# A heads' scores as three fp32r passes on row halves, a longer planned power in the opening, and new job orders

## The chip, the cores and the metric

One core of one Trainium2 chip runs the whole program. The metric is the device time of one execution in microseconds (us); lower is better. Engines are named as in the profile: PE is TensorE (its weight loads are listed apart as PEld), DVE is VectorE, ACT is ScalarE, POOL is GpSimd, SP is the engine that issues the DMAs here.

## What is computed

Two layers of a hybrid encoder on 256 rows of 1024 features, in fp32. Each layer mixes tokens by two kinds of attention with gates, then runs a squared-ReLU MLP. The change touches the scores of the first kind ("A": 8 query heads over 2 key heads, head dimension 64):

```python
def gqa_attention(q, k, v):
    ...
    q = q.reshape(B, S, Hkv, rep, hd)
    scale = hd ** -0.5
    def block(i):
        qi = lax.dynamic_slice_in_dim(q, i * Q_BLOCK, Q_BLOCK, axis=1)
        s = jnp.einsum('bqgrd,bkgd->bgrqk', qi, k, preferred_element_type=jnp.float32) * scale
        p = jax.nn.softmax(s, axis=-1).astype(v.dtype)
        return jnp.einsum('bgrqk,bkgd->bqgrd', p, v)

for l in range(DEPTH):
    ada = c_act @ w_ada[l] + b_ada[l]
    sh1, sc1, gt1, sh2, sc2, gt2 = [a[:, None, :] for a in jnp.split(ada, 6, axis=-1)]
    h = rms(x, g_mix[l]) * (1.0 + sc1) + sh1
    parts = jnp.split(h @ w_in[l], IN_SPLITS, axis=-1)
    qa = axial_rope(rms(qa, q_norm_a[l]), row_cs, col_cs)
    ka = axial_rope(rms(ka, k_norm_a[l]), row_cs, col_cs)
    y_a = gqa_attention(qa, ka, va) @ w_branch_a[l]
    ...
    x = x + gt1 * (mixed @ w_out[l])
    h2 = rms(x, g_mlp[l]) * (1.0 + sc2) + sh2
    x = x + gt2 * (jnp.square(jax.nn.relu(h2 @ w_ff1[l])) @ w_ff2[l])
```

## The kernel before

The program first records every operation with its engine, tiles and an assumed cost (`Plan.record`, `Plan.cost`, L259 to L330), then plays the list through a model of the engines (`Plan.run`, L427) and issues everything in the order of the planned start times (`Plan.issue`, L661). Each engine works its own list in that order; waits between engines are semaphores. So an assumed cost decides only the order, and where two operations of one engine stand, not how long they take.

Weights come by DMA in tiles of 128x1024 (`wr`, 7 buffers). Each is split into a high part, rounded to the type fp32r by an ACT copy, and a low part, the remainder, by a DVE subtraction (`split_next`, L815). A product of two such pairs is three fp32r matmuls, high*high, low*high and high*low (`mm3`, L837). Most of the large products run in this way.

A layer's mixer runs a list of jobs, a string `seq0` or `seq1` (L38, L39): `c` a chunk of the q, k, v projection with its normalisation and rotation (`qk_post`, L962), `u` and `v` one eighth each of the gates, `a` and `b` a step of attention A or B, `y` a quarter of A's output projection, and `w` one tile of the adaptive vectors `ada`. A `w` is one DMA of 512 KB into `wr` and one DVE reduction of 128x1024 with its accumulator read (`ada_tile`, L742); it has no work for PE. `ada_f0` and `ada_f1` say how many such tiles follow each block of the MLP.

`qk_post` ends with PE transposes of a chunk into PSUM, which one ACT copy writes into the tile of transposed queries and keys (`dst`). For A these are `qa` (half of a buffer of the class `b8`, which has 16 buffers, L41) and `ka`. `att_a_scores` (L1099) then multiplies: two pairs of heads j, two row blocks t and two halves g give eight fp32 matmuls in a group, each with 64 contracted rows (g picks partitions 0 to 63 or 64 to 127), 128 query columns as weights and 256 key columns moving. There are two such groups in each layer. The class `b8` holds the split weights too, so its buffers bound how far ahead weights are split.

In the opening, `step_x` (L1634) normalises the two row blocks: sums of squares, one DVE addition, a power -0.5 on POOL, then the scaling on ACT or DVE and PE transposes. A DVE addition ahead of the power is planned 400 ns longer than it is (`keep(HOLD)`).

Of the kernel before, what the change touches and what calls it, by code (L numbers as in the profile page):

```python
# [12 lines left out]
F32 = mybir.dt.float32  # L13
F32R = mybir.dt.float32r
BF16 = mybir.dt.bfloat16
AF = mybir.ActivationFunctionType
ALU = mybir.AluOpType
# [3 lines left out]
P = 128  # L21
D = 1024
S = 256
DEPTH = 2
HD = 64
# [8 lines left out]
CFG = dict(ahead0=1,  # L34
  post0=(5, 2, 1, 0), s2k=9, ahead=1, last="k",
  hk=2,
  ada_f0=[3, 1, 8, 2, 1, 6, 2, 4, 2], ada_f1=[2, 0, 0, 0, 0, 0, 0, 0, 0],
  seq0="w a v w v w w c3 c4 w w v a a w u u w w v a w w w w w b w v b w w w w w w w u y w y y y w w".split(),  # L38
  seq1="u w c4 v a w w w w w u a c3 w v a c5 u w w w w w w c2 w a w y y y y u b b v w w w w w w w w v w".split())  # L39
WR = 7  # L40
NB8 = 16  # L41
WARM = 5
# [114 lines left out]
class Plan:  # L157
# [101 lines left out]
    def record(self, e, op, a, k):  # L259
# [20 lines left out]
        o["port"] = from_sbuf and op != "reciprocal" and k.get("op") != ALU.pow and "reduce" not in op.replace("tensor_tensor_reduce", "")  # L280
        self.ops.append(o)

    @staticmethod
    def division(out, lhs):

        return ("row" if lhs.ap[0][1] == HD else "") + ("col" if out.ap[0][1] == HD else "")

    @staticmethod
    def cost(e, op, outs, ins, k):

        free = lambda z: int(np.prod([c for _, c in z.ap][1:]))
        n = max(free(z) for z in outs[:1] + ins)
        if e == "PE":
            n = free(outs[0])
            if op == "matmul" and F32R not in (ins[0].dtype, ins[1].dtype):
                if n > 256 and ins[0].ap[0][1] == P:
                    return 1.7 * n, 1.7 * n + 250.0
                cut = Plan.division(outs[0], ins[0])
                if not cut:
                    return 225.0, 475.0  # L300
                occ = max(0.4175 * n, 30.0) if cut == "rowcol" else 0.835 * n
                return occ, occ + 250.0
            occ = 228.5 if n > 256 else 120.5 if n > 128 else 109
            return occ, occ + 205
        if e == "SP":
            size = max(free(z) * mybir.dt.size(z.dtype) * z.ap[0][1] for z in outs)
            row = free(outs[0]) * mybir.dt.size(outs[0].dtype)
            return 480, size * (1.8 if ins[0].ap[0][0] == 0 else 1.6 if row < 4096 else 1.0)
        if e == "POOL":
            occ = 400 + 155 * n if k.get("op") == ALU.pow else 440 + 1.7 * n  # L310
            return occ, occ + (100 if n > 4 else 60)
        bank = "PSUM" in str(ins[0].space) if ins else False
        if e == "ACT":
            occ = (52 if bank else 93) + 0.834 * n
            occ += 96 * sum(pattern(k.get(z)) is not None for z in ("bias", "scale"))
            if k.get("accum_out") is not None:
                return occ + 93, occ + 308
            return occ, occ + 150
        if n <= 16:
            return 79, 204  # L320
        if op == "tensor_copy":
            occ = 69 + n / 0.96 if bank else 68 + n * 0.521
        elif op == "tensor_scalar":
            occ = (187 if bank else 135) + n * (1.04 if bank else 0.521)
        else:
            occ = 69 + n / 0.96
        if op == "tensor_tensor_reduce":
            return occ + 6, occ + 191
        return occ, occ + 125
# [366 lines left out]
def encoder(ctx: ExitStack, tc: tile.TileContext, a: dict, out: bass.AP):  # L696
# [5 lines left out]
    act, dve, pool, pe, sp = plan.lanes()  # L702
# [14 lines left out]
    def f32(t):  # L717
        return t.bitcast(F32)
# [243 lines left out]
    def qk_post(l, c, t, ps, nh, segs, axial, dst):  # L962
        n = nh * HD
        nm = f"{l}_{c}_{t}"

        qs = s2k(f"qs{nm}")[:, :n]
        act.activation(qs, ps[:, :n], AF.Copy)
        sq = s2k(f"sq{nm}")[:, :n]
        act.activation(sq, ps[:, :n], AF.Square)
        t1 = s2k(f"t1{nm}")[:, :n]  # L970
        t2 = s2k(f"t2{nm}")[:, :n]
        v3 = lambda z: z.rearrange("p (h d) -> p h d", d=HD)
        s0, ns = segs
        per = nh // ns
        tb = tabs_of[l]
        ct = tb[:, t, 0, s0 : s0 + ns, :]
        st = tb[:, t, 1, s0 : s0 + ns, :]
        v4 = lambda z: z.rearrange("p (s h d) -> p s h d", s=ns, d=HD)
        bc = lambda z, w: z[:, :, None, :].to_broadcast([P, ns, per, w])
        if axial:  # L980
            assert ns == 1
            w = HD // 4
            q5, o5 = (z.rearrange("p (h b s x) -> p h b s x", b=2, s=2, x=w) for z in (qs, t2))
            sv = st[:, 0, :].rearrange("p (b s x) -> p b s x", b=2, s=2)
            for s in range(2):
                (dve if l == 1 else pool).tensor_tensor(
                    o5[:, :, :, s, :], q5[:, :, :, 1 - s, :],
                    sv[:, None, :, s, :].to_broadcast([P, nh, 2, w]), op=ALU.mult,
                )
        else:  # L990
            w = HD // 2
            for s in range(2):
                (dve if l == 1 else pool).tensor_tensor(
                    v4(t2)[:, :, :, s * w : (s + 1) * w], v4(qs)[:, :, :, (1 - s) * w : (2 - s) * w],
                    bc(st[:, :, s * w : (s + 1) * w], w), op=ALU.mult,
                )
        r = tl("sbuf", [P, 8], F32, "rstd", 4, f"rstd{nm}")[:, :nh]
        dve.reduce_sum(r, v3(sq), axis=AX.X)
        with plan.together():
            dve.tensor_scalar(r, r, HD * EPS, None, op0=ALU.add)  # L1000
            dve.tensor_tensor(v4(t1), v4(ps[:, :n]), bc(ct, HD), op=ALU.mult)
        pool.tensor_tensor(r, r, half[:, :nh], op=ALU.pow)
        dve.tensor_tensor(t1, t1, t2, op=ALU.add)
        dve.tensor_tensor(v3(t1), v3(t1), r[:, :, None].to_broadcast([P, nh, HD]), op=ALU.mult)
        np_ = nh // 2
        tp = pt(f"qT{nm}")[:, : np_ * P]
        for j in range(np_):
            pe.transpose(tp[:, j * P : (j + 1) * P], t1[:, j * P : (j + 1) * P], ident)
        tv = tp.rearrange("p (j n) -> p j n", j=np_)
        act.activation(dst[:, :, t * P : (t + 1) * P], tv, AF.Copy)  # L1010

    def v_post(ps, dst):
        pv = ps.rearrange("p (h d) -> p h d", d=HD)
# [17 lines left out]
    def attention_tiles(l):  # L1031
        T = {}

        z = [tl("sbuf", [P, 2, 4, S], F32, "b8", NB8, f"qk{l}{i}") for i in range(2)]
        T["qa"] = z[0][:, 0]
        T["b", 0], T["b", 1], T["b", 2] = z[0][:, 1], z[1][:, 0], z[1][:, 1]
        T["ka"] = tl("sbuf", [P, 1, S], F32, "ka", 1, f"ka{l}")
        v = tl("sbuf", [P, 2, 16, HD], F32, "b8", NB8, f"v{l}")
        T["va"] = [v[:, t, 12:14] for t in range(2)]
        T["vb"] = [v[:, t, 0:12] for t in range(2)]  # L1040
        T["oa"] = Split([tl("sbuf", [P, 4, 2, S], F32R, "b8", NB8, f"oa{l}")], 4)
        T["ob"] = Split([tl("sbuf", [P, 4, 2, S], F32R, "b8", NB8, f"ob{l}")[:, :2]], 2)
        return T
# [55 lines left out]
    def att_a_scores(l, T, js):  # L1099

        sps = {(j, g): pa(f"sa{l}_{g}_{j}") for j in js for g in range(2)}
        with plan.together():
            for j in js:
                for t in range(2):
                    for g in range(2):
                        rows = slice(HD * g, HD * (g + 1))
                        q = T["qa"][rows, j, t * P : (t + 1) * P]
                        pe.matmul(sps[j, g][:, t * S : (t + 1) * S], q, T["ka"][rows, 0, :], start=True, stop=True)
        return sps

    def att_a_soft(l, j, sps, home):
# [522 lines left out]
    def step_x(t):  # L1634
        for c in range(2):
            sum_sq(0, 0, t, c, eng[f"ss{t}{c}"] == "d")
        ss = ss_of[0, 0, t]
        r = ss[:, 0:1]
        with plan.keep(HOLD):
            dve.scalar_tensor_tensor(r, r, EPS, ss[:, 1:2], op0=ALU.add, op1=ALU.add)  # L1640
        pool.tensor_tensor(r, r, half[:, :1], op=ALU.pow)
        for g in range(2):
            xn = s2k(f"xn00{t}{g}")
            xg = x[:, t, g * 512 : (g + 1) * 512]
            if eng[f"xn{t}{g}"] == "a":
                act.activation(xn, xg, AF.Copy, scale=r)
            else:
                dve.tensor_scalar(xn, xg, r, None, op0=ALU.mult)
            ps = pt(f"xT00{t}{g}")
            for k in range(4):  # L1650
                pe.transpose(ps[:, k * P : (k + 1) * P], xn[:, k * P : (k + 1) * P], ident)
            copy_by(
                eng[f"xT{t}{g}"], xT[:, 4 * g : 4 * g + 4, t * P : (t + 1) * P], ps.rearrange("p (k n) -> p k n", k=4)
            )
# [190 lines left out]
```

## Time and profile before

| | us |
|---|---|
| median of 3 runs (727.13 to 727.39) | 727.33 |
| the profiled execution, its own time | 726.78 |
| its span in the trace | 725.0 |
| PE busy | 720.1 |
| DVE busy | 584.6 |
| ACT busy | 466.9 |
| POOL busy | 65.6 |

The profiled execution took 726.78 us, 1.78 us of it outside the traced span, and lies 0.55 us under the median. Busy is the time in which at least one instruction of the engine is in flight; overlapping instructions count once. A group's mean is the time of one instruction from start to end, so for pipelined matmuls it is longer than the step from one to the next. Nearly all operations were recorded by one helper, so all stand under one line of code, L692, and the tile names tell them apart: `w` is a split weight, `hT` the transposed activations, `ka,qk` A's scores, `qk` B's scores, `s2k` a scratch tile, `ps` PSUM.

### The profile page before, as it was taken

The numbers are of one execution on the slowest core, as the hardware profiler recorded it, in microseconds if no ns is written. First come the engines' busy times: TensorE is split into PE (matmuls) and PEld (weight loads), VectorE is DVE, ScalarE is ACT, GpSimd is POOL, SyncE is SP. The second block draws the span as 40 slices with busy tenths as digits, with TensorE's granted clock in tenths as the row PEclk, the third lists the DMA queues.
The fourth block names the chain that finished last, engine by engine and source line by source line (L and its number), as shares of the span: only waits on it lengthen the run. The fifth ranks groups of instructions, "written<-read, shape, count | busy, mean of one in ns | idle before, by whom it ended". The sixth has DMA issues, their size and how long they took to land.

```text
span 725.0 us, 10593 instructions
## 1 busy us (share of the span) xinstructions
PE 720.1 (99%) x3844; PEld 599.6 (83%) x3844; DVE 584.6 (81%) x911; ACT 466.9 (64%) x791; POOL 65.6 (9%) x60
## 2 busy tenths in 40 slices
PE   9999999999999999999999999999999999999998
PEld 7787887788888888888888888878888888888887
DVE  6999999999899978774799979898799765456643
ACT  6569589875575766653476498658847766545540
POOL 1007460000000041000003101010000000000000
PEclk9999999999999999999999999999999999999999
DMA  9997758997499998785546777968476965566101
GB/s 352 407 407 247 247 184 292 344 391 224 148 333 398 384 350 285 278 297 186 203 149 228 263 221 268 332 225 299 147 235 225 335 210 166 170 230 212 50 0 59
DMA packets 50868, 180.95 MB, mean 250 GB/s; under 512 B 5728, under 2 KB 6784, under 8 KB 50816
## 3 DMA queue, kind: packets, MB, share of 16 engines
q1 hardware_dynamic: 50816, 180.28, 70.3%
q8 instruction: 30, 0.49, 0.3%
q14 instruction: 22, 0.18, 0.1%
HBM read 178.66 MB, written 1.06 MB: 248 GB/s over the span
## 4 chain that ended last, share of the span: by engine, by line
PE 92%; DVE 4%; DMA 1%; ACT 1%; issue 1%; POOL 0%; SPq 0%; ACTq 0%; DVEq 0%
PE ps L692 92%; DVE s2k L692 2%; DVE w L692 1%; DMA wr<-in_w_x 1%; DMA xin<-in_x 1%; ACT s2k L692 0%; ACT hT L692 0%; POOL ss L692 0%; ACT w L692 0%; DVE shg L692 0%; DVE w20wx L692 0%; DVE hT L692 0%; DVE xT L692 0%; DVE rstd L692 0%; DVE xin L692 0%
## 5 line engine op out<-in xcount | busy, mean ns | idle before, releaser
L692 DVE TENSOR_TENSOR w<-wr,w 128x1024 fp32r<-128x1024 f32 x234 | 282.1, 1226 | 44.1 <-ACT w L692 43.9
L692 ACT ACTIVATE w<-wr 128x1024 fp32r<-128x1024 f32 x234 | 242.0, 1057 | 86.9 <-PE ps L692 48.9
L692 PE MATMUL ps<-w,hT 128*128 128x512 f32 x1032 | 246.0, 394 | 0.3 <-DVE s2k L692 0.3
L692 PEld LDWEIGHTS ps<-w,hT 128*128 128x128 f32 x1032 | 190.8, 188 | 40.8 <-DVE s2k L692 0.7
L692 PE MATMUL ps<-w,hid 128*128 128x512 f32 (+1 forms) x780 | 176.0, 385 | 0.0
L692 PEld LDWEIGHTS ps<-w,hid 128*128 128x128 f32 x780 | 143.1, 188 | 28.3
L692 PE MATMUL ps<-hT,w 128*128 128x512 f32 (+1 forms) x896 | 158.6, 337 | 0.0
L692 PEld LDWEIGHTS ps<-hT,w 128*128 128x128 f32 x896 | 139.4, 190 | 18.7
L692 DVE CUSTOM_DVE_ANT_0 s2k<-wr,c_act 128x1024 bf16<-128x1024 f32 x96 | 116.7, 1226 | 3.3 <-DMA wr<-in_w_ada 3.3
L692 ACT ACTIVATE s2k<-ps 128x256 f32<-128x256 f32 (+3 forms) x108 | 45.0, 439 | 70.4 <-PE ps L692 70.2
L692 DVE TENSOR_TENSOR s2k<-ps,s2k 128x256 f32<-128x256 f32 x56 | 22.9, 419 | 32.2 <-ACT s2k L692 32.1
L692 PE MATMUL ps<-w,mT 128*128 128x512 f32 x192 | 45.7, 393 | 0.0
L692 ACT ACTIVATE s2k<-s2k 128x512 f32<-128x512 f32 (+1 forms) x62 | 38.5, 623 | 7.0 <-DVE s2k L692 6.1
L692 PEld LDWEIGHTS ps<-w,mT 128*128 128x128 f32 x192 | 35.5, 188 | 7.4 <-DVE mT L692 0.3
L692 POOL TENSOR_TENSOR rstd<-rstd,half 128x8 f32<-128x8 f32 (+1 forms) x20 | 31.5, 1577 | 98.4 <-DVE rstd L692 98.1
L692 DVE TENSOR_TENSOR hid<-s2k,hid 128x512 fp32r<-128x512 f32 x28 | 19.3, 688 | 18.8 <-ACT hid L692 18.8
L692 ACT ACTIVATE pr<-pr,st 128x256 f32<-128x256 f32 (+1 forms) x64 | 32.5, 568 | 2.9 <-DVE st L692 2.9
L692 POOL TENSOR_TENSOR ss<-ss,half 128x1 f32<-128x1 f32 x8 | 5.8, 727 | 259.4 <-DVE ss L692 259.4
L692 PEld LDWEIGHTS ps<-xin,s2k 128*128 128x128 f32 x180 | 20.9, 140 | 7.1 <-issue 1.6
L692 PE MATMUL ps<-xin,s2k 128*128 128x128 f32 x180 | 26.2, 275 | 0.5 <-ACT s2k L692 0.5
L692 DVE TENSOR_TENSOR s2k<-ps,gtb 128x512 f32<-128x512 f32 (+1 forms) x18 | 11.7, 658 | 18.4 <-PE ps L692 18.4
L692 POOL TENSOR_TENSOR s2k<-s2k,tabs 128x256 f32<-128x256 f32 (+1 forms) x20 | 18.0, 919 | 52.7 <-ACT s2k L692 52.5
(106 smaller groups left out, 506.8 us busy)
## 6 DMA issues: line engine op xcount, KB each, us to landing
wr<-in_w_ff SPq DMA_DIRECT2D x120, 512.0 KB, 4.9
wr<-in_w_ada SPq DMA_DIRECT2D x96, 512.0 KB, 5.3
wr<-in_w_gate SPq DMA_DIRECT2D x32, 512.0 KB, 5.1
wr<-in_w_qkv SPq DMA_DIRECT2D x24, 512.0 KB, 4.8
wr<-in_w_x SPq DMA_DIRECT2D x16, 512.0 KB, 5.8
wr<-in_w_out SPq DMA_DIRECT2D x16, 512.0 KB, 5.5
wr<-in_w_y SPq DMA_DIRECT2D x8, 512.0 KB, 5.5
wr<-in_w_ba SPq DMA_DIRECT2D x8, 512.0 KB, 5.4
```

The lines of the kernel that those rows point to most:

```text
L692: getattr(self.real[o["e"]], o["op"])(*map(real, o["a"]), **{n: real(z) for n, z in o["k"].items()})
```

## The change

Three edits, and new job lists. First, A's queries and keys are stored as high and low fp32r parts: after the ACT copy of the transposes (now into fp32r) a DVE subtraction writes the remainder, and each score matmul becomes three fp32r matmuls, alternating between the two halves. `qa` becomes a whole `b8` buffer of its own, where it was half of one; the second half of `qk`'s second buffer stands empty. Second, the plan takes 61 ns for an fp32r matmul on part of the array, and 900 ns more for the power of the second row block in the opening. Third, the lists of jobs differ: `seq0` has 24 `w` in place of 25, `ada_f0` sums to 26 in place of 29, `seq1` has 29 in place of 24, `ada_f1` 1 in place of 2. In `seq0` the two `b` stand with two `w` between them, where a `w` and a `v` stood.

```diff
@@ CFG
-  ada_f0=[3, 1, 8, 2, 1, 6, 2, 4, 2], ada_f1=[2, 0, 0, 0, 0, 0, 0, 0, 0],
-  seq0="w a v w v w w c3 c4 w w v a a w u u w w v a w w w w w b w v b w w w w w w w u y w y y y w w".split(),
-  seq1="u w c4 v a w w w w w u a c3 w v a c5 u w w w w w w c2 w a w y y y y u b b v w w w w w w w w v w".split())
+  ada_f0=[4, 1, 9, 3, 1, 2, 0, 5, 1], ada_f1=[1, 0, 0, 0, 0, 0, 0, 0, 0],
+  seq0="w a v v w w c3 c4 w w a v u a w w v a w w u w w b w w b w w v w w w w w w w y y w y w y u".split(),
+  seq1="w u w w c4 w w v a u w a c3 w w w w v w a w w w c5 u c2 a w u w y w w y y w y w w w w b b v v w w w w w w".split())
@@ Plan
+    def slow_power(self, ns):
+
+        o = self.ops[-1]
+        o["occ"], o["lat"] = o["occ"] + ns, o["lat"] + ns
+
@@ Plan.cost
             occ = 228.5 if n > 256 else 120.5 if n > 128 else 109
+            if op == "matmul" and Plan.division(outs[0], ins[0]):
+                occ = 61.0
             return occ, occ + 205
@@ qk_post
-        act.activation(dst[:, :, t * P : (t + 1) * P], tv, AF.Copy)
+        if dst.shape[1] == 2 and len(dst.shape) == 4:
+            hi, lo = (dst[:, i, :, t * P : (t + 1) * P] for i in range(2))
+            act.activation(hi, tv, AF.Copy)
+            dve.tensor_tensor(lo, tv, f32(hi), op=ALU.subtract)
+        else:
+            act.activation(dst[:, :, t * P : (t + 1) * P], tv, AF.Copy)
@@ attention_tiles
-        T["qa"] = z[0][:, 0]
-        T["b", 0], T["b", 1], T["b", 2] = z[0][:, 1], z[1][:, 0], z[1][:, 1]
-        T["ka"] = tl("sbuf", [P, 1, S], F32, "ka", 1, f"ka{l}")
+        T["b", 0], T["b", 1], T["b", 2] = z[0][:, 0], z[0][:, 1], z[1][:, 0]
+        T["qa"] = tl("sbuf", [P, 2, 4, S], F32R, "b8", NB8, f"qa{l}")
+        T["ka"] = tl("sbuf", [P, 2, 1, S], F32R, "ka", 1, f"ka{l}")
@@ att_a_scores
-                    for g in range(2):
-                        rows = slice(HD * g, HD * (g + 1))
-                        q = T["qa"][rows, j, t * P : (t + 1) * P]
-                        pe.matmul(sps[j, g][:, t * S : (t + 1) * S], q, T["ka"][rows, 0, :], start=True, stop=True)
+                    for n, (u, v) in enumerate(((0, 0), (1, 0), (0, 1))):
+                        for g in range(2):
+                            rows = slice(HD * g, HD * (g + 1))
+                            q, k = T["qa"][rows, u, j, t * P : (t + 1) * P], T["ka"][rows, v, 0, :]
+                            pe.matmul(sps[j, g][:, t * S : (t + 1) * S], q, k, start=n == 0, stop=n == 2)
@@ step_x
         pool.tensor_tensor(r, r, half[:, :1], op=ALU.pow)
+        if t == 1:
+            plan.slow_power(900.0)
```

## Rows read from the trace of the kernel before

**Rows 1.** Page, part 1: engine, busy us (share of the span), instructions
```profile
PE 720.1 (99%) x3844; PEld 599.6 (83%) x3844; DVE 584.6 (81%) x911; ACT 466.9 (64%) x791; POOL 65.6 (9%) x60
```
**Rows 2.** Chain that ended last, its end: start us, us, what
```profile
57.21 0.69 DVE s2k L692
57.90 0.04 issue
57.95 663.97 PE ps L692 x3584
```
**Rows 3.** Waits of PE from 58 us on: us in total, times, longest
```profile
PE ps L692 <- DVE s2k L692: 0.3, 1, 0.3
```
**Rows 4.** Timeline of PE, first score group: start us, us, instruction, count
```profile
82.89 1.18 PE L692 MATMUL ps<-w,hT 128*128 128x512 f32 x4
84.00 2.00 PE L692 MATMUL ps<-ka,qk 64*128 64x256 f32 x16
85.93 0.96 PE L692 MATMUL ps<-w,hT 128*128 128x512 f32 x3
...
84.53 1.25 PE L692 MATMUL ps<-ka,qk 64*128 64x256 f32 x10
```
**Rows 5.** Groups by form, whole span: busy us, mean ns of one
```profile
L692 PE MATMUL ps<-ka,qk 64*128 64x256 f32 x64 | 8.0, 389 | 0.0
...
L692 ACT ACTIVATE qk<-ps 128x512 f32<-128x512 f32 x16 | 9.4, 599 | 7.4 <-PE ps L692 7.3
...
L692 DVE TENSOR_TENSOR mT<-ps,mT 128x512 fp32r<-128x512 f32 x8 | 5.3, 681 | 0.0
...
L692 ACT ACTIVATE mT<-ps 128x512 fp32r<-128x512 f32 x8 | 4.7, 597 | 3.6 <-PE ps L692 3.5
...
L692 PEld LDWEIGHTS ps<-s2k,xin 64*128 64x128 f32 x16 | 1.1, 187 | 0.4
...
L692 DVE TENSOR_TENSOR s2k<-ps,tabs 128x128 f32<-128x128 f32 x4 | 1.1, 280 | 0.0
```
**Rows 6.** Timeline of PE, fp32r matmuls of 256 columns on the whole array
```profile
211.39 2.30 PE L692 MATMUL ps<-hT,w 128*128 128x512 f32 x17
213.53 0.86 PE L692 MATMUL ps<-w,hid 128*128 128x512 f32 x3
```
**Rows 7.** Timeline of PE's weight loads in the opening, fp32 on halves
```profile
8.34 0.42 PEld L692 LDWEIGHTS ps<-s2k,xin 64*128 64x128 f32 x6
```
**Rows 8.** Busy time by stretch: window, its us, PE, PEld, DVE, ACT, POOL, clock, DMA
```profile
58.00:126.00 68.00, 68.00 (x371) 55.23 (x375) 67.14 (x110) 54.96 (x120) 31.12 (x28) 1.00 0.72 238
126.00:160.00 34.00, 34.00 (x275) 26.78 (x268) 32.77 (x63) 27.84 (x51) 0.00 (x0) 1.00 0.96 364
160.00:190.00 30.00, 30.00 (x145) 24.66 (x144) 28.65 (x44) 17.91 (x28) 0.56 (x1) 1.00 0.72 232
380.00:440.00 60.00, 60.00 (x290) 49.40 (x289) 53.45 (x97) 40.68 (x79) 12.65 (x8) 1.00 0.72 244
440.00:520.00 80.00, 80.00 (x526) 64.61 (x525) 67.95 (x120) 59.43 (x113) 3.37 (x3) 1.00 0.74 261
```
**Rows 9.** Waits of ACT, whole span: us in total, times, longest
```profile
ACT w L692 <- PE ps L692: 48.9, 31, 3.9
```
**Rows 10.** Timelines of the opening: POOL's powers, DVE beside them, ACT behind
```profile
7.34 1.02 POOL L692 TENSOR_TENSOR ss<-ss,half 128x1 f32<-128x1 f32 x1 [6.90 <-DVE ss L692]
9.02 1.47 POOL L692 TENSOR_TENSOR ss<-ss,half 128x1 f32<-128x1 f32 x1 [0.67 <-DVE ss L692]
...
8.86 1.22 DVE L692 CUSTOM_DVE_ANT_0 s2k<-wr,c_act 128x1024 bf16<-128x1024 f32 x1
...
10.53 1.34 ACT L692 ACTIVATE s2k<-xin,ss 128x512 f32<-128x512 f32 x2 [0.44 <-POOL ss L692]
```
**Rows 11.** Busy time of the opening's stretch, columns as in rows 8
```profile
4.00:54.00 50.00, 49.47 (x234) 39.40 (x234) 45.81 (x87) 32.71 (x49) 2.49 (x2) 1.00 1.02 408
```
**Rows 12.** Timelines of PE, attention B's scores: one of layer 0's two, layer 1's
```profile
137.14 1.56 PE L692 MATMUL ps<-qk 64*64 64x256 f32 x48
...
493.86 2.89 PE L692 MATMUL ps<-qk 64*64 64x256 f32 x96
```

## The prediction

> **What bounds the kernel now.** I read the page's busy times first, then the end of the chain of waits, then PE's waits, then busy time by stretch. PE is busy 720.1 of 725.0 us [rows 1], the chain's last 664 us are PE alone with no other engine between [rows 2], and from 58 us on PE waits once, 0.3 us [rows 3]. So time is saved only where PE's own work gets shorter, or before 58 us. The view by stretch warns of a second limit. In layer 0's attention, 58 to 190 us, DVE is busy 67.14 of 68, 32.77 of 34 and 28.65 of 30 us: 3.44 us are left. In layer 1's, 380 to 520 us, 18.6 of 140 are left [rows 8]. The opening, 4 to 54 us, has its DMA engines full (a share of 1.02 at 408 GB/s) beside a PE busy 49.47 of 50 [rows 11].
>
> **The scores, PE's part.** A group is 16 records for eight fp32 matmuls, and from its first start to that of the next matmul 1.93 us pass [rows 4]. Inside, ten records last 1.25 us and one lasts 0.389 [rows 4, 5]; so their starts lie within 0.86 us, and taken as five pairs (one per half at a time) that is 4 steps of 0.215 us. Eight pairs take 1.72 us; the other 0.21 us is the change to the halves, which the new group pays too, as do its neighbours. The new group has 24 fp32r matmuls, 12 pairs. No row shows fp32r on halves. On the whole array, the first of the 17 matmuls takes up to 0.227 us of the 2.14 from its start to the next line's, and the 16 fp32r matmuls of 256 columns behind it take 0.12 each [rows 6]. If the halves run side by side as they do in fp32, a pair takes 0.12 and the group 1.44: 0.28 saved. There are four groups (64 records [rows 5]): 1.1 us. The bounds: half of fp32's step, 0.108, saves 1.7 us; a pair that stays at fp32's 0.215 because something other than the moving columns sets it costs 12 x 0.215 - 1.72 = 0.86 a group, 3.4 us more than before. I take 0.12, since it is the same type and the same columns.
>
> What could hold the step at 0.215 is the loading of weights, since each short matmul brings a load of its own. In the opening, six loads of 64 rows by 128 columns last 0.42 us and one lasts 0.187 [rows 5, 7]: starts within 0.23 us, three pairs, two steps of 0.11 us. So two loads a step of 0.11 are possible, in fp32. The Trainium skill, on the page "TensorE: Matmul & The Clock Gate", section "LDWEIGHTS (loading the stationary operand)", speaks against the change here: a load costs columns / 1.2 ns whatever the number of rows, an estimate of 107 ns for 128 columns, and if the two loads of a pair ran one behind the other, that would be 213 ns a pair: the scores would take as long as the second rival below says, and the sum would be its 730.6 us. The 0.11 us step disagrees with loads in a row, and for fp32r on halves no run here shows it.
>
> **The remainders, DVE's part.** `qk_post` runs twice (t) for the q chunk and twice for the k chunk in each layer. Its ACT copy into fp32r costs what the fp32 copy costs (597 and 599 ns [rows 5]). New are four subtractions of 128x512 at 681 ns, from the same form, and four of 128x128 at 280 ns, the nearest form [rows 5]: 3.84 us of DVE, 1.92 in each layer. In layer 0 one `w` fewer takes its reduction away, 1.22 us [rows 10]. Net 0.7 us for a DVE with 3.44 us left over 132 us [rows 8]. Each subtraction also holds its PSUM bank for its time and DVE's queue ahead of it, and behind it queue weight subtractions that PE waits for. Layer 1 gets 1.92 us and five more `w`, 6.1 us, into 18.6 us of room: free. The tiles moved out of layer 0's MLP only lighten it there; each brings its 512 KB DMA on SP's queue along, and the DMA share in both attentions is 0.72 to 0.96. PE's price of the DVE work: between 0 and 1.92 us (all of layer 0's, if nothing of it is hidden); I take 0.2, since the net 0.7 is a fifth of the room.
>
> **The buffer.** `qa` takes one of 16 `b8` buffers more while A runs. Over the whole span ACT's weight copies wait 48.9 us for PE to release such tiles [rows 9], and PE doesn't starve for it [rows 3]; a buffer fewer makes the lead shorter by one tile. Bounds 0 and 1 us (a fraction of ACT's longest wait, 3.9); I take 0.
>
> **The power.** The second power takes 1.47 us against 1.02 for the first, with a DVE reduction of 1.22 us started 0.16 us ahead of it; ACT stands idle 0.44 us for it, with its next copy queued behind [rows 10]. Planned longer, it lets ACT put another copy into that hole, which is worth at most 0.44 us there. But behind it the opening is paced by full DMA engines [rows 11], so most is given back before 58 us. Gain 0.1; bounds 0.4 gained and 0.4 lost, if the new order serves the wrong block first.
>
> **The order of jobs.** It adds and removes no PE work, only changes between forms. Layer 1's two `b` stand together and their scores ran as one group of 2.89 us; layer 0's run as two of 1.56 [rows 12]: 0.23 us apart, less a tail counted twice, plus an entry and an exit. With no PE job between layer 0's two `b` now, they may join: 0.2 us. Other groups of transposes may join or part, by 0.5 us either way.
>
> **Sum.** -1.1 (scores) + 0.2 (DVE) + 0 (buffer) - 0.1 (power) - 0.2 (order) = -1.2 us. Against the profiled execution that is 725.6 us, span 723.8; against the median, which is what a new median is compared with, 727.33 - 1.2 = 726.1 us.
>
> **Rivals.** First, DVE becomes the bound in layer 0: PE, which waits nowhere there now, waits for weight remainders or scores. For it: under 3% of DVE is free from 58 to 126 us. Against it: its `w` reductions can slide. Price up to 1.92 + 0.2: it gives 727.33 - 1.4 + 1.9 = 727.8 us. Second, the slower one: a pair of fp32r matmuls on halves doesn't go below fp32's 0.215 us, by its loads or because the halves don't overlap in this type. It decides from 0.143 us a pair on (1.72 / 12), and gives 727.33 + 3.4 - 0.1 = 730.6 us. For it: no such row exists, and a pass now has a load of its own for half the columns' time. Against it: the 0.11 us step of loads. Third, the change doesn't do what it says in the opening: the 900 ns were right only beside that one reduction, and the new order there has ACT or DVE serve something else first. It loses 0.4 and the joins don't come either: 727.33 - 1.1 + 0.2 + 0.4 = 726.8 us, or up to 727.8.
>
> **How the numbers follow.** My forecast, 0.72: 726.1 us, its own range 724.6 (the low ends of scores, power and order together, not quite reached) to 727.4. DVE as the bound 0.13, halves that don't overlap 0.08, the opening 0.07. A measurement of this kernel tells about 0.2%, 1.45 us, from no change: faster means under 725.9, just beside the forecast. Of the forecast's 0.72 I put 0.40 under it and 0.32 above; DVE and the opening fall nearly whole within 0.2% (0.19 of 0.20), the overlap rival above: faster 0.40, same 0.51, slower 0.09. The range, 724.6 to 728.0, takes in the forecast's own and the first and third rivals, and leaves out the second and the tails.
>
> **What would show it.** In the changed profile: `ka,qk` with 96 records in groups of about 1.65 us (1.44 and 0.21); eight new DVE subtractions into `qk` and `ka` tiles at 681 and 280 ns; PE still with no wait beyond 0.5 us from 58 us on; ACT's 0.44 us hole in the opening gone; one B score group in layer 0. Groups over 1.93 us would bring down the first step, PE waits on DVE between 58 and 190 us the second.

## The result and the profile after

The changed kernel takes 729.48 us (median of 7 runs, 728.99 to 730.22) against 727.37 us of the kernel before on the same chip (7 runs, 727.04 to 727.6): ratio 1.003, 95% interval 1.002 to 1.004. It is slower by 0.3%, 3.4 us above the forecast and 1.5 us outside its range. The profiled execution took 730.22 us with a span of 728.4, the longest of the seven; medians are compared with medians below, and places in the traces with places.

The page of the kernel after, parts 1 and 4, answers to [rows 1, 2]:

```profile
PE 719.4 (99%) x3876; PEld 599.0 (82%) x3876; DVE 591.7 (81%) x919; ACT 466.7 (64%) x791; POOL 71.4 (10%) x60
...
PE 78%; DVE 10%; DMA 4%; ACT 4%; issue 3%; POOL 1%; SPq 0%; DVEq 0%; ACTq 0%
```

PE's busy time fell by 0.7 us, DVE's rose by 7.1, of which 3.7 are the new remainders below. The chain that ended last was PE alone from 57.95 us on [rows 2]; now a tenth of it is DVE. PE's waits from 58 us on (us in total, times, longest), against the single 0.3 of [rows 3]:

```profile
PE ps L699 <- DVE s2k L699: 2.5, 3, 1.4
PE ps L699 <- DVE rstd L699: 0.3, 1, 0.3
```

The three waits of the first row end at 97.10 us (1.45), 110.30 (0.55) and 166.43 (0.51). None stands ahead of the first scores.

The first score group of A and layer 0's score group of B, timeline of PE (start, us, count), answer to [rows 4, 12]:

```profile
86.92 1.68 PE L699 MATMUL ps<-ka,qa 64*128 64x256 f32 x24
88.53 4.38 PE L699 MATMUL ps<-w,hT 128*128 128x512 f32 x18
...
131.83 2.89 PE L699 MATMUL ps<-qk 64*64 64x256 f32 x96
```

From 86.92 to 88.53 are 1.61 us, where the old group took 1.93. The other three groups take 1.56 to 1.62. So the scores give back 1.3 us in four groups, and layer 0's B scores ran as one group. Both were forecast.

The new remainders and the copies ahead of them, groups by form (busy us, mean ns):

```profile
L699 DVE TENSOR_TENSOR qa<-ps,qa 128x512 fp32r<-128x512 f32 x4 | 2.7, 686 | 0.4 <-ACT qa L699 0.4
L699 ACT ACTIVATE qa<-ps 128x512 fp32r<-128x512 f32 x4 | 2.4, 600 | 6.2 <-PE ps L699 6.2
L699 DVE TENSOR_TENSOR ka<-ps,ka 128x128 fp32r<-128x128 f32 x4 | 1.0, 281 | 0.0
```

They cost by themselves what the rows of before said, 0.68 and 0.28 us each. The longest of PE's waits stands behind them, from 95.65 to 97.10 us. First POOL's powers (min, median, max in ns), then who waits, then the two waiting rows of DVE and PE:

```profile
L699 POOL TENSOR_TENSOR rstd<-rstd,half x2: 1637/2889/4141, 90.5 to 92.1; 128x8 f32<-128x8 f32 x2
...
96.26 0.69 DVE L699 TENSOR_TENSOR s2k<-s2k,rstd 128x512 f32<-128x512 f32 x1 [1.53 <-POOL rstd L699]
...
97.10 0.63 PE L699 MATMUL ps<-xin,s2k 128*128 128x128 f32 x4 [1.45 <-DVE s2k L699]
```

The second power of chunk c3 took 4.14 us where the first took 1.64. DVE waited 1.53 us for it, and PE 1.45 us for DVE.

In the opening, ACT's hole of 0.44 us [rows 10] is gone and the first product of k=0 started 0.6 us earlier (14.22 for 14.83). But PE then waited at k=2, for which nothing stood before:

```profile
26.32 0.73 PE L699 MATMUL ps<-w,hT 128*128 128x512 f32 x2 [1.55 <-ACT hT L699]
```

### The profile page after: what moved, and what is told of

It is laid out like the page before. It is cut to its first block, busy times and chain, and to the rows that moved or that the text cites. A ratio compares the mean times of both kernels' runs of the same rounds, so it can differ in the third digit from the quotient of the medians.

```text
span 728.4 us, 10654 instructions
## 1 busy us (share of the span) xinstructions
PE 719.4 (99%) x3876; PEld 599.0 (82%) x3876; DVE 591.7 (81%) x919; ACT 466.7 (64%) x791; POOL 71.4 (10%) x60
## 4 chain that ended last, share of the span: by engine, by line
PE 78%; DVE 10%; DMA 4%; ACT 4%; issue 3%; POOL 1%; SPq 0%; DVEq 0%; ACTq 0%
PE ps L699 78%; DVE s2k L699 5%; DVE w L699 3%; DMA wr<-in_w_ada 2%; ACT pr L699 1%; DMA wr<-in_w_bb 1%; DVE rstd L699 1%; POOL rstd L699 1%; DMA xin<-in_x 1%; ACT w L699 1%; ACT s2k L699 1%; ACT hT L699 0%; DMA wr<-in_w_gate 0%; DVE shg L699 0%; DVE st L699 0%
## 5 line engine op out<-in xcount | busy, mean ns | idle before, releaser
L699 POOL TENSOR_TENSOR rstd<-rstd,half 128x8 f32<-128x8 f32 (+1 forms) x20 | 34.0, 1705 | 94.6 <-DVE rstd L699 93.9
```

What stands on the lines that cost most here:

```text
L699: getattr(self.real[o["e"]], o["op"])(*map(real, o["a"]), **{n: real(z) for n, z in o["k"].items()})
```

## Experiments

One table by stage places the gains and losses of every kernel, from the starts of three products in its profile: the first behind the opening (57.95 us before, the start of the chain's last piece [rows 2]), the first of layer 0's MLP (201.84 us before), and the last of all. "Layer 0" is the stretch between the first two, "rest" that from the second to the third. The opening ends between 58.25 and 58.57 in eight variants; before's own 57.95 is an early one. Every row of the table is one profiled execution: three kernels run the same opening (after, after with no remainders in layer 0, after with one power earlier), and their ends differ by up to 0.7 us.

| kernel | median, us | opening ends | layer 0 | rest |
|---|---|---|---|---|
| before | 727.23 to 727.37 | 57.95 | 143.89 | 519.78 |
| after | 729.48 | 59.55 | 145.85 | 519.66 |
| power only | 730.19 | 58.36 | 146.69 | 519.78 |
| scores only | 728.82 | 58.49 | 146.25 | 519.10 |
| job lists only | 727.66 | 58.53 | 143.79 | 520.02 |
| after without the power | 728.69 | 58.57 | 145.36 | 519.61 |
| scores in layer 1 only | 726.66 | 58.55 | 143.82 | 519.13 |
| after, no remainders in layer 0 | 727.06 | 58.86 | 142.85 | 519.68 |
| after, k=2 put back in the opening | 729.28 | 59.17 | 145.19 | 519.66 |
| after, one power earlier | 727.76 | 59.42 | 143.56 | 519.64 |
| before, one copy ahead | 727.25 | 58.41 | 143.85 | 519.84 |
| before's order, remainders added | 728.80 | 58.25 | 145.36 | 519.80 |
| the same, one remainder first | 729.09 | 58.35 | 145.94 | 519.80 |

### The parts alone

The kernel before with the longer planned power alone:

```diff
+    def slow_power(self, ns):
+        o = self.ops[-1]
+        o["occ"], o["lat"] = o["occ"] + ns, o["lat"] + ns
@@ step_x
+        if t == 1:
+            plan.slow_power(900.0)
```

> The kernel before with only the longer planned power. In the changed kernel's profile PE stands 1.55 us at the second weight tile of the opening and is 1.6 us later than before at the opening's end. Theory O (the new order of the opening makes the loss): this run shows that stall and is about 1.5 us slower than before, 728.8 us. Theory D (the stall is the DMA of that one execution, which landed late whatever the order): no stall over 0.5 us there, time within 0.5 us of before. Theory L (layer 0's attention is where it goes: DVE and POOL too tight) has nothing to lose here: within 0.5 us of before.

Measured: 730.19 us (4 runs), ratio 1.0042 (1.0025 to 1.0059). None of the three theories had this. No instruction is added, and the opening ends as in the others; the loss, 2.8 us, lies in layer 0, where the plan put everything in another order. PE's waits there, in a kernel that does the work of before:

```profile
PE ps L697 <- DVE w L697: 0.7, 2, 0.5
PE ps L697 <- DVE s2k L697: 0.5, 2, 0.2
PE ps L697 <- ACT hT L697: 0.2, 1, 0.2
```

By this view they add up to 1.4 of the 2.8 us. The view counts from the modelled end of the matmul ahead, so it shows less than is lost: the first score group takes 2.25 us to the start of the next matmul (85.33 to 87.58) in place of 1.93, for a listed wait of 0.25. Where the rest of the other half went was not found. It shows what a plan made anew can cost here.

The scores alone (before's lists and power, remainders and fp32r scores in both layers, and the 61 ns in the plan):

```diff
@@ CFG (against the change)
-  seq0="w a v v w w c3 c4 w w a v u a w w v a w w u w w b w w b w w v w w w w w w w y y w y w y u".split(),
+  seq0="w a v w v w w c3 c4 w w v a a w u u w w v a w w w w w b w v b w w w w w w w u y w y y y w w".split(),
...
@@ step_x
-        if t == 1:
-            plan.slow_power(900.0)
```

> The kernel before with only the three fp32r passes (with their planned 61 ns, the remainders on DVE and the buffer of their own), with the old job lists and the old planned power. All theories: score groups of about 1.61 us, as in the changed kernel. Theory L: PE waits for DVE or POOL in layer 0's attention, 2 to 3 us together, and the run is 1 to 2 us slower than before, 728.5 to 729.5 us. Theory O: no such waits beyond 0.5 us, and the run is about 1 us faster than before, 726.3 us.

Measured: 728.82 us, ratio 1.0023 (1.0013 to 1.0032). The rest of the program gains 0.68 us, which is layer 1's two groups; layer 0 loses 2.4. The whole loss is in the layer where DVE was full. The time is theory L's, but its 2 to 3 us of waits aren't there:

```profile
PE ps L699 <- DVE s2k L699: 0.8, 3, 0.4
```

Of these 0.8 us, 0.26 stand at the opening's end and 0.54 in layer 0. Where the rest of the loss lies was not found, and since this order was planned anew, as in the run with the power alone, the run doesn't tell the remainders' own cost from that of the new order.

The job lists alone (fp32 scores, before's power):

```diff
@@ CFG (against before)
-  ada_f0=[3, 1, 8, 2, 1, 6, 2, 4, 2], ada_f1=[2, 0, 0, 0, 0, 0, 0, 0, 0],
+  ada_f0=[4, 1, 9, 3, 1, 2, 0, 5, 1], ada_f1=[1, 0, 0, 0, 0, 0, 0, 0, 0],
...
```

> The kernel before with only the new job lists; the scores stay fp32. Theory L, if it is the extra DVE work that does it: no long waits in layer 0, time within 0.5 us of before. Rival to it, theory J (the new job lists themselves leave too little lead): waits of 1 us and more in layer 0's attention here too, 728.5 us or more. Theory O: as before, within 0.5 us.

Measured: 727.66 us, ratio 1.0008 (0.9999 to 1.0018): not told apart from no change, and theory J (728.5 or more) falls. Layer 0 gains 0.1 us, the rest loses 0.24. Layer 0's B scores did not join here, though the list is the changed kernel's:

```profile
119.61 0.89 PE L692 MATMUL ps<-qk 64*64 64x256 f32 x24
...
129.98 2.22 PE L692 MATMUL ps<-qk 64*64 64x256 f32 x72
```

The change without its power edit:

```diff
-        if t == 1:
-            plan.slow_power(900.0)
```

> The changed kernel with the power planned as before. Theory O: the opening's stall of 1.55 us goes, and the run is about 1.5 us faster than the changed kernel, 728.0 us, the scores' 1.3 us still eaten in layer 0. Theory L alone: the opening plays no part, 729.3 us as the changed kernel.

Measured: 728.69 us, ratio 1.002 (1.001 to 1.0029), 0.8 us under the changed kernel, between theory O's 728.0 and theory L's 729.3. So the power costs 3.0 us alone and 0.8 on top of the others: the parts don't add up, and each of these plans is a new order.

### Where DVE has no room

The scores in layer 1 only; layer 0 keeps its fp32 scores and, on all engines, before's order:

```diff
@@ attention_tiles, att_a_scores
+        if l == 0:
+            T["qa"] = z[0][:, 0]
...
+        else:
...
+            T["qa"] = tl("sbuf", [P, 2, 4, S], F32R, "b8", NB8, f"qa{l}")
+            T["ka"] = tl("sbuf", [P, 2, 1, S], F32R, "kb", 1, f"ka{l}")
```

> The kernel before, old job lists and old power, with the three fp32r passes in layer 1 alone; in layer 0 all five engines keep the order of before. Theory L (the loss is layer 0's, where DVE is full): layer 1 has room for the remainders, so nothing is lost and the scores of layer 1 give 0.6 us (two groups, 0.32 each) or more: 726.0 to 726.7 us. Theory J (any new plan of the order costs 1 to 3 us, wherever): layer 1 is planned anew here too, and PE waits there: 727.5 us or more.

Measured: 726.66 us (11 runs), ratio 0.999 (0.9981 to 0.9999). Layer 0 stays at 143.82, the rest gains 0.65 us, and nothing is lost for the remainders, where DVE has room [rows 8]: theory L. It is the fastest kernel of this study, faster than both.

The changed kernel in its own order, instruction for instruction, without layer 0's four remainder subtractions; its low passes there read the high parts:

```diff
@@ Plan.issue
             for o in order:
+                if o.get("skip"):
+                    continue
```

> The changed kernel with its order kept operation for operation, except that layer 0's four remainder subtractions are left out and its score matmuls take the high parts in all three passes (so layer 0's scores lack their low parts). 1.9 us of DVE work goes from 60 to 90 us, nothing else. Theory L (the DVE work itself): PE's waits between 90 and 166 us, 3.2 us together in the changed kernel's profile, shrink by 1.5 us or more: 728.0 us or less. Theory J (the order, which has no room whatever DVE's load): they stay within 0.5 us: 729.0 us or more.

Measured: 727.06 us (theory L), 2.4 us under the changed kernel for 1.92 us of DVE work left out. Layer 0 takes 3.0 us less in the traces. The waits of 1.45 us ahead of 97 us and of 0.51 ahead of 166 are gone, that at 110 fell from 0.55 to 0.29, and the second power of c3 took 1.80 us in place of 4.14:

```profile
L701 POOL TENSOR_TENSOR rstd<-rstd,half x2: 1639/1719/1799, 89.3 to 90.9; 128x8 f32<-128x8 f32 x2
...
86.24 1.68 PE L701 MATMUL ps<-ka,qa 64*128 64x256 f32 x24
```

The first scores start 27.38 us behind the opening's end (86.24 less 58.86); in the changed kernel, with all four remainders, it is 27.37 (86.92 less 59.55). Up to the scores that order takes in the remainders at no cost, and all of the 2.4 us is lost behind them.

The opposite of it: the kernel before in its own order, with layer 0's remainders and fp32r scores put in.

```diff
@@ Plan.issue (before)
+                for z in [z for z in late if z[0] <= start[o["i"]] or "part" in o]:
...
+                    self.real["DVE"].tensor_tensor(part, of, high.bitcast(F32), op=ALU.subtract)
+                if "low" in o:
...
+                    self.real["ACT"].activation(out.bitcast(F32R), of, *o["a"][2:], **o["k"])
+                    late.append((start[o["i"]] + o["lat"] + 200.0, o["low"]))
+                if "part" in o:
...
+                                self.real["PE"].matmul(*map(real, z[n]), start=n == 0, stop=n == 2)
```

> The kernel before in its own planned order, instruction for instruction; only in layer 0 the four remainder subtractions (two of 128x512, two of 128x128, 1.92 us of DVE) are added behind their ACT copies, and the eight fp32 score matmuls of each group become 24 fp32r ones. Layer 1 keeps fp32 scores. For want of memory the four remainders go to one scratch of half their size, one over the other, and all copies of queries and keys are rounded to fp32r, so the low passes multiply wrong numbers; the work is the changed kernel's. PE's part saves 2 x 0.32 us. Theory L (in layer 0 DVE has no usable room, so its work costs PE as much, in whatever order): 728.0 to 728.8, with new waits of PE on DVE between 84 and 190 us. Theory T (the 3.4 us of room take it as long as the order that was fitted to it stays, and what the changed kernel loses it loses by its new order): 726.5 to 727.1, and no new wait over 0.3 us.

Measured: 728.80 us, ratio 1.002 (1.0011 to 1.003), theory L at its upper end. The scores save their 0.6 us and the kernel loses 1.4 all the same, so 1.92 us of DVE work cost 2.1 in an order that nothing else had touched. Both waits stand at the first score group, on PE's timeline:

```profile
83.86 0.66 PE L717 MATMUL ps<-xin,s2k 128*128 128x128 f32 x4 [0.84 <-DVE s2k L717]
...
86.75 0.39 PE L714 MATMUL ps<-ka,low 64*128 64x256 f32 x2 [0.98 <-DVE low L699]
```

The first is for a DVE that has three of the remainders behind it by then (0.28, 0.28 and 0.68 us), and that also stood still for a power on POOL:

```profile
74.61 0.82 DVE L717 TENSOR_TENSOR s2k<-s2k,rstd 128x128 f32<-128x128 f32 x1 [0.59 <-POOL rstd L717]
```

The second is the last remainder, which stood behind a weight subtraction of 1.22 us. Whether that place is the cause was asked by swapping those two:

```diff
+            copy = next(o for o in order if o.get("nm") == "0_0_1")
+            w = [o for o in order[: order.index(copy)] if o["e"] == "DVE"][-1]
+            order.remove(w)
+            order.insert(order.index(copy) + 1, w)
```

> The kernel of the run before (old order, layer 0's remainders added), with one DVE instruction moved: the weight remainder of 128x1024 (1.22 us) that stood ahead of the last query remainder now stands behind it, so that the scores behind 85 us no longer wait 0.98 us for it. Theory P (what the remainders cost is their place, the wait of one late one): the wait falls under 0.3 us, nothing takes its place, and the time falls by 0.7 to 1.0 us, to 727.8 to 728.1. Theory L (DVE is late as a whole there, so the weight remainder, now 0.9 us later, or the next operation is waited for instead): less than 0.4 us is gained, 728.4 or more.

Measured: 729.09 us, ratio 1.0024 (1.0013 to 1.0035), so nothing came back: theory L. The wait that was aimed at fell from 0.98 to 0.17 us, and the last row lists PE's waits on DVE from 58 us on:

```profile
86.01 0.39 PE L720 MATMUL ps<-ka,low 64*128 64x256 f32 x2 [0.17 <-DVE low L703]
...
PE ps L723 <- DVE s2k L723: 1.4, 3, 0.8
```

Of the 1.4 us, 0.80 are the first wait of the run before, and 0.36 are a new one that ends at 106.84 us; where the rest of what the swap gained was lost again was not found. So the place of this one remainder was not the cause. That before's order has no room there fits the view by stretch of the kernel before, cut at the first scores (columns as in [rows 8]):

```profile
58.00:84.00 26.00, 26.00 (x123) 21.05 (x123) 25.82 (x42) 17.64 (x35) 15.78 (x16) 1.00 0.72 223
84.00:110.00 26.00, 26.00 (x138) 21.12 (x139) 25.57 (x41) 22.51 (x49) 15.34 (x12) 1.00 0.66 217
```

All four remainders fall due by the scores at 84 us, and up to there DVE was idle for 0.18 us of 26. This holds for that order and not for the layer. Four `w` reductions stand in these 26 us (at 67.73, 76.50, 80.05 and 81.80 us), while PE waits for nothing; no run moved them alone. The changed kernel has three ahead of its first scores (65.93, 78.33 and 84.20 us), and takes the remainders there at no cost.

### The stretched power

The changed kernel, with the first row block's addition and power of chunk c3 two DVE sums earlier, so that POOL begins the second power 0.9 us sooner:

```diff
@@ Plan.issue
+        for k in ("pow ", "add "):
+            o = order.pop(at(k + "0_3_0"))
+            order.insert(at("sum 0_3_0") + 1, o)
```

> The changed kernel, with two instructions moved and all else in its order: the DVE addition and the POOL power of the first row block of chunk c3 in layer 0 stand right behind their sum, two DVE sums earlier. There the second block's power took 4.14 us where one took 1.64, beside DVE operations that read two SBUF tiles; DVE then waited 1.53 us for it and PE 1.45 us. Moved, the second power starts some 1 us earlier, before or at the head of that row of DVE operations. Theory Z (the stretched power costs what PE waited behind it): the second power takes at most 2.6 us, PE's wait at about 95 us falls under 0.3 us, and the time falls by 1.0 to 1.6 us, to 727.9 to 728.5. Theory D (DVE has too little room in layer 0 whatever this power does, so the wait comes back at the next operation that needs DVE): the wait at 95 us may go, but 729.0 or more stays. Theory R (the power is starved for as long as such DVE operations follow one another, wherever it starts): it takes 4 us or more again and the time stays within 0.3 us of 729.4.

Measured: 727.76 us (11 runs), ratio 1.0006 (0.9997 to 1.0015), 1.7 us under the changed kernel, for two small instructions moved: theory Z, a little under its range. The power took its 1.64 us, and DVE's row went on without the hole:

```profile
91.22 1.64 POOL L707 TENSOR_TENSOR rstd<-rstd,half 128x8 f32<-128x8 f32 x1 [0.88 <-DVE rstd L707]
...
93.52 1.21 DVE L707 TENSOR_TENSOR w<-wr,w 128x1024 fp32r<-128x1024 f32 x1
94.65 0.68 DVE L707 TENSOR_TENSOR s2k<-s2k,rstd 128x512 f32<-128x512 f32 x1
```

So the wait was the largest single piece of the loss, and it did not come back elsewhere; that at 166 us went with it, and 0.52 us stay at 108.66. This kernel has all four remainders, and is only 0.7 us slower than the one without them (727.06). The 2.4 us are thus 1.7 for the stretched power and 0.7 for the rest.

That a late DVE makes the power long is not shown. Beside it the same DVE operations run in the same order with the remainders (first two lines behind the power) and without them (last two):

```profile
92.09 4.14 POOL L699 TENSOR_TENSOR rstd<-rstd,half 128x8 f32<-128x8 f32 x1
...
91.73 1.26 DVE L699 TENSOR_TENSOR s2k<-s2k,s2k 128x512 f32<-128x512 f32 x2
...
93.52 1.21 DVE L699 TENSOR_TENSOR w<-wr,w 128x1024 fp32r<-128x1024 f32 x1
...
90.52 1.28 DVE L701 TENSOR_TENSOR s2k<-s2k,s2k 128x512 f32<-128x512 f32 x2
...
92.33 1.21 DVE L701 TENSOR_TENSOR w<-wr,w 128x1024 fp32r<-128x1024 f32 x1
```

The power starts 0.36 us behind the first of these operations with the remainders and 0.37 without, and takes 4.14 us there and 1.80 here.

Why the power took 4.14 us was asked twice with small programs that compute nothing of the encoder. First, a power of 128x8 beside rows of DVE operations of different kinds:

```diff
+    pool.tensor_tensor(r[i + 1], q[i], half, op=ALU.pow)
+    for n, kind in enumerate(stream):
+        if kind == "s":
+            dve.tensor_tensor(o, x[:, 0, 0:512], x[:, 0, 512:], op=ALU.add)
+        elif kind == "p":
+            dve.tensor_tensor(o, ps, x[:, 0, 512:], op=ALU.mult)
...
```

> None of the encoder is computed; the output is a copy of x. Eight powers of 128x8 on POOL one after the other, beside DVE streams of 128x512 fp32: none, one, two and four additions of two SBUF tiles, four products of a PSUM and an SBUF tile, four copies, four sums over SBUF, none. Theory S (POOL's access waits until DVE leaves off, however many operations that are): 1.64 us alone, about 0.6, 1.2 and 2.4 us more for one, two and four additions. Theory W (it waits for the one operation in flight alone, as the plan has it): never over 2.4 us. For products with PSUM, copies and sums both leave it open; nearer to 1.64 us if one SBUF input leaves room.

```profile
3.12 1.64 POOL L36 TENSOR_TENSOR r<-q,half 128x8 f32<-128x8 f32 x1 [0.28 <-DVE q L35]
6.32 2.01 POOL L36 TENSOR_TENSOR r<-q,half 128x8 f32<-128x8 f32 x1 [1.57 <-DVE q L35]
8.61 2.01 POOL L36 TENSOR_TENSOR r<-q,half 128x8 f32<-128x8 f32 x1 [0.28 <-DVE q L35]
11.10 1.64 POOL L36 TENSOR_TENSOR r<-q,half 128x8 f32<-128x8 f32 x1 [0.48 <-DVE q L35]
```

Beside two or four additions out of SBUF it takes 2.01 us, beside products out of PSUM the 1.64 that it takes alone (sums 1.64, copies 1.74). This is theory W. With one addition DVE's operation came behind the power, so that case tells nothing. Second, the start of the power was shifted against longer rows:

```diff
+    for n in range(3, 9):
+        pool.tensor_tensor(m[:, :n], q[:, :n], half[:, :n], op=ALU.pow)
+        pool.tensor_tensor(r, q, half, op=ALU.pow)
+        dve.tensor_tensor(y[:, 0], ps, x[:, 0, 512:], op=ALU.mult)
...
```

> Nothing of the encoder is computed; the output is a copy of the input. Twelve trials: on POOL a power of 128 x n (n = 3 to 8, so the next one starts some 0.15 us later each time) and behind it a power of 128 x 8; on DVE meanwhile a product out of PSUM and then a row of operations on two SBUF tiles: six additions in the first six trials, and in the other six two additions, a product with a broadcast, a subtraction of 128x1024 into fp32r and an addition, as they stand around 92 us in the changed kernel. Alone the power takes 1.64 us. Theory W (it waits for the DVE operation in flight at most): every second power takes 1.64 to 2.3 us. Theory P (it depends on the moment of its start against the DVE operations: it slips in or is held up to the end of the row): some take 1.64 to 2.3 us and others 3.5 us or more, and those end some 1.64 us behind the end of DVE's row. Theory R (held whenever such a row runs): all take 3 us or more.

```profile
16.43 1.64 POOL L44 TENSOR_TENSOR r<-q,half 128x8 f32<-128x8 f32 x1
21.04 2.04 POOL L44 TENSOR_TENSOR r<-q,half 128x8 f32<-128x8 f32 x1
...
47.41 2.10 POOL L44 TENSOR_TENSOR r<-q,half 128x8 f32<-128x8 f32 x1
```

All twelve took 1.64 to 2.10 us, theory W: each ends 1.49 to 1.53 us behind the end of the DVE operation in flight at its start, as if it waited for that one alone. The 4.14 us did not come; that power ends 1.50 us behind the end of the fourth operation (94.73 us), as if it waited for the whole row. Why it was held there stays open; the phase alone, as far as it was varied here, is not the cause. It is no accident of one execution: the kernel with k=2 put back (below), which has the same order there, shows it again:

```profile
L708 POOL TENSOR_TENSOR rstd<-rstd,half x2: 1637/2891/4145, 90.1 to 91.7; 128x8 f32<-128x8 f32 x2
```

### The opening

The changed kernel with k=2 of the opening in before's order:

```diff
+        self.moves = [("sc2", "lo x2"), ("h2", "hi y2"), ("i2", "hi y2"), ("j2", "lo y2")]
...
+        for what, of in self.moves:
+            ahead(what, of)
```

Here `sc2` is the small DVE operation on the adaptive vector of k=2, `h2`, `i2` and `j2` the two scalings and the remainder of its activations, and `hi` and `lo` are splits of a weight tile.

> The changed kernel with its order kept, but at the opening's second weight tile a small DVE operation is put back ahead of a weight split that waits for a DMA, and on ACT and DVE the activations of that tile ahead of the next split, as before had it. Theory O (this order makes the opening's stall): the wait of 1.55 us at 24 us falls under 0.6 us and the run is 0.8 to 1.4 us faster than the changed kernel, 728.1 to 728.7 us. Theory D (it is when the DMA lands): stall and time stay, 729.5 us.

Measured: 729.28 us, 0.2 us under the changed kernel. The wait at k=2 fell to 0.34 us, as theory O had it, and the opening still ended at 59.17 and the time stayed, as theory D had it; so that wait is not what the opening loses. And the kernel before, with one ACT copy moved into the hole in front of the second power:

```diff
+        o = order.pop(at("xT00"))
+        order.insert(at("xn10"), o)
```

> The kernel before, with one ACT instruction moved: the copy xT00 of the first transposes goes ahead of the scaling that waits for the second power, into the hole of 0.44 us. It is what the longer planned power does to ACT first; nothing else of the order changes. Theory G (the opening is paced by its DMAs, so what is gained is given back): ACT's hole is gone, the first product of k=0 starts 0.3 to 0.7 us earlier, the opening ends within 0.2 us of where it did, 727.0 to 727.6. Theory E (the gain is kept): 726.7 to 727.0. Theory C (the opening's edit by itself costs what the run with the power alone lost): 728.5 or more.

Measured: 727.25 us (11 runs), ratio 1.0 (0.9991 to 1.0009): theory G. The hole is filled; the first product of k=0 starts 0.3 us earlier (14.50), and the opening ends where it does in its neighbours:

```profile
10.14 0.60 ACT L699 ACTIVATE xT<-ps 128x512 f32<-128x512 f32 x1
10.67 1.34 ACT L699 ACTIVATE s2k<-xin,ss 128x512 f32<-128x512 f32 x2
```

The gain is given back before 58 us. The changed kernel's opening loses 0.3 to 1.0 us against the latest of the others, and only where the power's edit stands together with the new scores and lists: alone it ends at 58.36, without it at 58.57. So it comes with that order; which instruction of it, the one swap didn't show.

## Why the prediction was wrong

**What bounds the kernel** was read rightly: PE from 58 us on, the opening by its DMAs, DVE as the second limit in layer 0.

**The scores** were right: 0.28 us a group forecast, 0.32 measured, 1.3 us in all for 1.1. Its step of 0.12 us holds: 1.61 us less the 0.21 for the change to the halves are 1.40 for twelve pairs, 0.117 each, a little under the row from the whole array. The rival with a step of 0.215 falls. The Trainium skill's rule on the page "TensorE: Matmul & The Clock Gate", section "LDWEIGHTS (loading the stationary operand)", counted as two loads in a row for each pair, would have made it an estimated 213 ns; the trace disagrees, with some 117 ns for a pair and its two loads.

**The remainders** are the step that failed. 1.92 us of DVE work in layer 0, net 0.7 after one `w`, was priced at 0.2 us of PE's time, at most 1.92, because DVE had 3.44 us left over 132 us. In the changed kernel leaving them out gives 2.4 us, and in before's order putting them in costs 2.1: both above the upper bound of the term. The idle share of the stage told neither price. In before's order DVE had 0.18 us left up to where the remainders fall due, and with them added PE waited there 0.84 and 0.98 us. In the changed order the remainders cost nothing up to the first scores, where one `w` less stands ahead of them. There 1.7 of the 2.4 us is PE's wait behind one power of POOL that took 4.14 us in place of 1.80, and 0.7 the rest. The upper bound failed because it held DVE's own work only, and no term for what another engine's late result does to DVE. The size is in part luck: the same remainders cost 0.7 us or 2.4 as that one power runs on or is held, and what holds it is open. A price of 0.2 was too low in each of the three.

**The buffer**: no wait of PE for it shows, as forecast; no run tested it alone.

**The power**: 0.1 us gained, bounds 0.4 either way. The local part of the step was right, the hole closes and the gain is given back, as the moved copy shows (0.0 us). What was missing is that a planned duration changes the order of everything behind it. Alone that cost 3.0 us, on top of the rest 0.8, in both cases outside the bounds. The third rival had the mechanism but looked no further than the opening; in the changed kernel the opening did lose, some 0.8 us for the rival's 0.4.

**The order of jobs**: 0.2 us gained, bounds 0.5. The B scores joined in the changed kernel (one group of 2.89 us for two of 1.56); no run shows what that is worth alone, since with the job lists alone they did not join. The lists by themselves gained 0.1 us in layer 0 and lost 0.24 behind it, within the bounds.

**The rivals.** The first, DVE as the bound in layer 0, came nearest: PE waits for it there. Its price of 727.8 us was too low by 1.7, the wait behind the stretched power, which it didn't hold. That the kernel without this wait takes 727.76 us doesn't confirm it; that agreement is luck, since that kernel's layer 0 is 0.3 us shorter than before's and its loss lies in the opening. The rival's chance, 0.13, was small for a DVE that was over 97% busy in that layer.

**The sum, as measured**, in the changed kernel: the scores -1.3; layer 0's remainders +2.4, of which the stretched power is 1.7; the opening some +0.8 (58.86 to 59.55 in the four kernels that have its order, one of them with k=2 put back, 59.25 on average, against 58.25 to 58.57, 58.44 on average). Those make +1.9 of the +2.1. The rest of 0.2 is not split among the parts. It hides two larger ones: from layer 0's MLP on, the kernel without layer 0's remainders takes 519.68 us where the new scores in the old lists take 519.10 and 519.13, some 0.5 more, of which the lists alone show 0.24; and its layer 0 is some 0.4 shorter than before's less the scores' 0.64.

## What to carry to other kernels

Work for a nearly full engine is not priced by the idle share of a whole stage: cut the view by stretch from when its input is there to when its result is due, and where the engine is idle for less than the new work, let the bounds reach beyond the work itself, since what it shifts can hold others up. Here the same 1.92 us cost 2.1 us in one order, 2.4 in another and 0.7 in that one with two small instructions moved by two places. A saving on PE that hands work to DVE belongs where DVE has room: in layer 1 alone the new scores gave 0.7 us, in both layers, with a plan made anew, they lost 1.6. Where a planner sorts the whole program, a changed cost or list is an edit to every order behind it, with a range of some 3 us of its own here.

## What the runs showed of the hardware that was not expected

A power of 128x8 on POOL takes 1.64 us alone, and as long beside DVE operations that read PSUM, or sums; beside rows of operations on two SBUF tiles it takes up to 2.10 us in a small program and 2.6 at other places of these kernels, as here in the kernel before, and 4.14 us at one place of the changed kernel, again in another execution of the same order.

```profile
94.34 2.63 POOL L692 TENSOR_TENSOR rstd<-rstd,half 128x8 f32<-128x8 f32 x1
...
94.23 1.24 DVE L692 TENSOR_TENSOR w<-wr,w 128x1024 fp32r<-128x1024 f32 x1
```

The long ones end some 1.5 us behind the end of a DVE operation: of the one in flight at their start (95.48 us here, the power ends at 96.97), or, for the 4.14 us, of the fourth in the row (94.73 and 96.23). What decides between one operation and the whole row is open.
